# Where a kernel's tiles begin in SBUF: a constants tile wider by 32 bytes, and the t tiles in a pool of their own

## The chip, the cores and the metric

One core of one Trainium2 chip. The metric is the device time of one execution in microseconds (us). Three executions of the kernel before took 2665.67 to 2668.98 us, median 2666.57 us.

## What is computed

Two layers of one trunk. In each layer 256 latent rows and 256 context rows of 2048 channels are normalised and modulated, and one large projection feeds four mixers side by side. Cut to what matters:

```
for l in range(DEPTH):                                   # DEPTH = 2
    hx = modulate(rmsnorm(x, pre_g[l]), shift_x, scale_x)     # 256 x 2048
    hc = modulate(rmsnorm(ctx, pre_g[l]), shift_c, scale_c)   # 256 x 2048
    px = split_proj(hx @ w_in[l])                             # 2048 -> 14144 columns
    pc = split_proj(hc @ w_in[l])        # last layer: only the 320 columns of the keys
    ...                                  # latent attention, 2-D DFT, short convolution, gMLP
    br = jnp.einsum('bngw,gwd->bngd', ys, w_branch)           # 4 branches, 512 -> 2048
    merged = jnp.sum(sigmoid(gates) * br, axis=2)
    out = merged @ w_out                                      # 2048 -> 2048
    x = x + gate_x * rmsnorm(out, post_g[l])
```

Inputs and outputs are float32. The modulation vectors come from a further product of silu(c) and silu(c_ctx) with w_mod (2048 x 6144 per layer).

## The kernel before

Nearly all the time goes to matrix products with 128 x 512 tiles of weights. A weight is streamed from HBM in chunks of 256 rows by 512 columns (`raw`, 512 KB, issued on SP's queue, line 235). For each half of a chunk, ScalarE rounds the float32 numbers to float32r (`wh`, line 245) and VectorE subtracts to get the rest (`wl`, line 246). The inputs are kept split in the same way: `hh` and `hl` are 16 + 16 tiles of 128 x 512 that hold the modulated input, and `y` and `m` tiles hold the inputs of the smaller products. Each product is then the sum of three float32r matmuls: high by high, low by high, high by low. They are written in one place:

```
if mode == "f":
    c = slice(j * P, (j + 1) * P)
    mm(b, wh[kk][:, c], xh, start=first, stop=False)      # line 272
    mm(b, wh[kk][:, c], xl, start=False, stop=False)      # line 273
    mm(b, wl[kk][:, c], xh, start=False, stop=last)       # line 274
else:
    mm(b, xh, wh[kk], start=first, stop=False)            # line 276
    mm(b, xl, wh[kk], start=False, stop=False)            # line 277
    mm(b, xh, wl[kk], start=False, stop=last)             # line 278
```

The second argument of `mm` is the stationary operand, 128 columns of which are loaded into the array before the matmul (the weight loads, PEld). The third is the moving operand, whose 512 columns (256 or 320 in a few products) are streamed through it. So in mode "f" the input moves and the weights stand; in mode "t" the weights move and the input stands. Lines 502 to 504 are the same triple in mode "t" for cq and kv of layer 0, which are computed by quarters while the modulation is still being worked out. Layer 0 runs mostly in mode "f" (up to about 1700 us), layer 1 mostly in mode "t".

Float32 matmuls that aren't split (transposes against an identity, attention scores at lines 717 and 718, the modulation's own products at line 337) use operands of `cst`, `t`, `s`, `m` and `raw`.

The SBUF tiles are taken from pools, in this order:

```
pc, pv, pw, pb, ps = pool("pc"), pool("pv"), pool("pw"), pool("pb"), pool("ps", space=PSUM)
```

`pc` holds the constants, one tile `cst` of 1796 float32 columns (7184 bytes in each partition). `pv` holds small vectors. `pw` holds `raw` (5 buffers), `wh` (6) and `wl` (5). `pb` holds `s`, `g`, `m`, `t`, `y`, `hh`, `hl` and one accumulator `ma`, in this order. A tile lies at the same bytes of every partition, each buffer is rounded up to 32 bytes, and the next follows without a gap. So the size of everything ahead of a tile decides where it begins. One of the three `t` buffers must hold a tile with a border for the convolution, 4 x 2 x 258 columns, so each `t` buffer has 8256 bytes, 64 more than a multiple of 256.

Of the kernel before, what the change touches and what calls it, by code (L numbers as in the profile page):

```python
# [17 lines left out]
F32 = mybir.dt.float32  # L18
# [5 lines left out]
PSUM = bass.MemoryType.PSUM  # L24

P = 128
# [128 lines left out]
def backbone(ctx: ExitStack, tc: tile.TileContext, a, out):  # L155
    nc = tc.nc
    pool = lambda n, b=1, **k: ctx.enter_context(tc.tile_pool(name=n, bufs=b, **k))
    pc, pv, pw, pb, ps = pool("pc"), pool("pv"), pool("pw"), pool("pb"), pool("ps", space=PSUM)
    pd = pool("pd", space=bass.MemoryType.DRAM)

    mm = nc.tensor.matmul
# [3 lines left out]

    def big(tag, shape, dt=F32):
        n = {"m": 4, "y": 2, "t": 3}[tag]
        return pb.tile(shape, dt, tag=tag, name=tag, bufs=n)

    def small(shape, dt=F32):  # L170
        return pb.tile(shape, dt, tag="s", name="s", bufs=4)
# [144 lines left out]
    def mod_products(l, part, k0, nk):  # L316
# [4 lines left out]
        for s in range(KD // 4):  # L321
            off = moff[l][part * D + k0 * P] + s * 4 * P * n
            if n < W:
                raw = pw.tile([P, KC, W], F32, tag="raw", name="raw", bufs=NR).rearrange("p k n -> p (k n)")
            elif s % 2 == 0:
                raw = big("y", [P, 2048])
            else:
                raw = None
            if raw is not None:
                nc.sync.dma_start(raw.rearrange("p (c f) -> p c f", c=2),  # L330
                                  a[f"wm{l}"][off:off + 4 * P * n].rearrange("(c p f) -> p c f", c=2, p=P))
                rows = [raw[:, i * n:(i + 1) * n] for i in range(4)]
            else:
                two = [raw_chunk(a[f"wm{l}"], off + i * KC * P * n) for i in range(2)]
                rows = [two[i // KC][:, i % KC, :] for i in range(4)]
            for i in range(4):
                mm(b[i * 32:(i + 1) * 32, :], cvz[:, s * 4 + i, :], rows[i], start=s == 0, stop=s == KD // 4 - 1,  # L337
                   tile_position=(0, i * 32))
            yield
# [87 lines left out]

    nc.sync.dma_start(vecs[0], a["vec0"])
    ncst = sum(n for _, n in CONST.values())
    cst = pc.tile([P, ncst], F32, name="cst")  # L430
    nc.sync.dma_start(cst[:, :2 * P + 4], a["const"][:, :2 * P + 4])
    K = {n: cst[:, s:s + w] for n, (s, w) in CONST.items()}
    ident = K["ident"]
# [1 line left out]
    sinT = K["sinT"].rearrange("p (t n) -> p t n", t=2)  # L435

    xs = [big("m", [P, 4, 512]) for _ in range(4)]
    rows_of = {}
    for v, src in enumerate((a["x"], a["ctx"])):
        for i in range(2):  # L440
            rows_of[v, i] = x = big("y" if v + i == 2 else "t", [P, D])
            nc.sync.dma_start(x, src[i * P:(i + 1) * P, :])
# [104 lines left out]
        pending = to_modulate(k0, nk)  # L547
    for _ in pending:
        pass
    nc.sync.dma_start(cst[:, 2 * P + 4:], a["const"][:, 2 * P + 4:])  # L550
    nc.sync.dma_start(vecs[1], a["vec1"])
    for _ in products:
        pass
# [613 lines left out]
```

## Time and profile before

| | us |
|---|---|
| median of three executions | 2666.57 |
| the profiled execution | 2668.45 |
| its span, first to last instruction | 2666.6 |
| TensorE busy (PE) | 2613.7 |
| VectorE busy (DVE) | 1583.2 |
| ScalarE busy (ACT) | 1028.6 |

The profiled execution is 1.9 us above its span. A matmul's duration in the trace is its own latency, from its start to its modelled end; the next one starts before it ends. So durations of matmuls overlap, and the pace of TensorE is read from the starts of matmuls that follow each other, not from their durations. That distance from start to start is called the pitch below. At the full clock of 2.4 GHz, 512 columns take 213.3 ns.

### The profile page before, as it was taken

Reading aid. Unit: us, or ns where it says so; the run is one execution under the profiler, and the core shown is the slowest. Engines: PE = TensorE matmul, PEld = TensorE weight load, DVE = VectorE, ACT = ScalarE, POOL = GpSimd, SP = SyncE. Lnnn points to the kernel's source line nnn. Section 1 sums busy time; section 2 is a strip of 40 time slices with the busy share of each in tenths; the row PEclk is TensorE's granted clock in tenths of the full one; section 3 lists DMA queues with packets and bytes.
Section 4 is the critical chain, followed back from the end, with each engine's and each line's share of the span. In section 5 each row is a group of like instructions: output and inputs, shape, how many; then the busy total and the mean of one; then the engine's idle time right before and its main releaser. Section 6 shows DMA issues by size and latency. Waiting matters only on the chain.

```text
span 2666.6 us, 33124 instructions
## 1 busy us (share of the span) xinstructions
PE 2613.7 (98%) x11803; PEld 2103.3 (79%) x11803; DVE 1583.2 (59%) x3000; ACT 1028.6 (39%) x1881; POOL 11.7 (0%) x25
## 2 busy tenths in 40 slices
PE   6899999999999999999999999999999999999998
PEld 3578787888888888888888888789788888888886
DVE  4377555656666566754554336776555555656666
ACT  4234432222222222222222235565555444544554
POOL 0000000000000000000000000000000000000000
PEclk9999999999999999999999999999999999999999
DMA  8854234444444444444444226754445555566565
GB/s 304 324 184 142 80 111 142 153 148 150 149 147 148 141 150 150 146 155 158 150 163 145 93 92 210 247 172 137 140 150 174 189 192 194 184 207 199 185 218 205
DMA packets 127350, 448.62 MB, mean 168 GB/s; under 512 B 13920, under 2 KB 19216, under 8 KB 125264
## 3 DMA queue, kind: packets, MB, share of 16 engines
q1 hardware_dynamic: 124944, 433.11, 48.4%
q0 software_dynamic: 2240, 13.40, 1.4%
q8 instruction: 92, 1.51, 0.2%
q14 instruction: 74, 0.61, 0.1%
HBM read 442.23 MB, written 4.22 MB: 167 GB/s over the span
## 4 chain that ended last, share of the span: by engine, by line
PE 96%; DVE 2%; issue 1%; DMA 1%; ACT 0%; SPq 0%; DVEq 0%; ACTq 0%
PE acc L272 16%; PE acc L273 16%; PE acc L274 16%; PE acc L278 13%; PE acc L276 13%; PE acc L277 13%; PE acc L502 1%; PE acc L504 1%; PE acc L503 1%; PE acc L337 1%; PE mis L421 1%; PE mis L717 1%; PE mis L718 1%; DVE m L1075 0%; DMA raw<-in_wm 0%
## 5 line engine op out<-in xcount | busy, mean ns | idle before, releaser
L246 DVE TENSOR_TENSOR wl<-raw,wh 128x512 fp32r<-128x512 f32 (+1 forms) x1256 | 848.3, 682 | 764.8 <-PE acc L274 349.0
L245 ACT CAST wh<-raw 128x512 fp32r<-128x512 f32 (+1 forms) x1256 | 767.7, 615 | 1359.7 <-PE acc L273 818.0
L272 PE MATMUL acc<-hh,wh 128*128 128x512 f32 x1536 | 614.7, 400 | 0.6 <-DVE m L837 0.6
L273 PE MATMUL acc<-hl,wh 128*128 128x512 f32 x1536 | 607.4, 395 | 0.0
L274 PE MATMUL acc<-hh,wl 128*128 128x512 f32 x1536 | 607.2, 395 | 0.0
L276 PE MATMUL acc<-wh,hh 128*128 128x512 f32 (+1 forms) x1440 | 566.2, 393 | 0.0
L278 PE MATMUL acc<-wl,hh 128*128 128x512 f32 (+1 forms) x1440 | 559.6, 389 | 1.1 <-DVE wl L246 1.0
L277 PE MATMUL acc<-wh,hl 128*128 128x512 f32 (+1 forms) x1440 | 558.6, 388 | 0.0
L361 DVE SCALAR_TENSOR_TENSOR ma<-raw,cv,ma 128x512 f32<-128x512 f32 x420 | 298.2, 746 | 131.0 <-DMA raw<-in_wm 130.1
L272 PEld LDWEIGHTS acc<-hh,wh 128*128 128x128 f32 x1536 | 288.7, 188 | 72.1 <-issue 1.9
L273 PEld LDWEIGHTS acc<-hl,wh 128*128 128x128 f32 x1536 | 288.7, 188 | 70.1 <-issue 1.9
L274 PEld LDWEIGHTS acc<-hh,wl 128*128 128x128 f32 x1536 | 288.6, 188 | 69.6
L278 PEld LDWEIGHTS acc<-wl,hh 128*128 128x128 f32 x1440 | 270.5, 188 | 60.1 <-DVE wl L246 3.5
L277 PEld LDWEIGHTS acc<-wh,hl 128*128 128x128 f32 x1440 | 270.7, 188 | 56.8 <-issue 1.9
L276 PEld LDWEIGHTS acc<-wh,hh 128*128 128x128 f32 x1440 | 270.6, 188 | 56.0 <-issue 1.9
L272 PE MATMUL acc<-y,wh 128*128 128x512 f32 x256 | 101.7, 397 | 0.0
L273 PE MATMUL acc<-y,wh 128*128 128x512 f32 x256 | 101.2, 395 | 0.0
L274 PE MATMUL acc<-y,wl 128*128 128x512 f32 x256 | 101.2, 395 | 0.0
L502 PE MATMUL acc<-wh,hh 128*128 128x512 f32 (+1 forms) x128 | 48.4, 381 | 11.9 <-ACT wh L245 7.3
L274 PEld LDWEIGHTS acc<-y,wl 128*128 128x128 f32 x256 | 48.1, 188 | 11.6
L272 PEld LDWEIGHTS acc<-y,wh 128*128 128x128 f32 x256 | 48.1, 188 | 11.5
L273 PEld LDWEIGHTS acc<-y,wh 128*128 128x128 f32 x256 | 48.1, 188 | 11.5
(229 smaller groups left out, 1680.3 us busy)
## 6 DMA issues: line engine op xcount, KB each, us to landing
raw<-in_wi SPq DMA_DIRECT2D x432, 512.0 KB, 3.5
raw<-in_wm SPq DMA_DIRECT2D x168, 512.0 KB, 4.2
raw<-in_wo SPq DMA_DIRECT2D x104, 512.0 KB, 4.2
raw<-in_wb SPq DMA_DIRECT2D x64, 512.0 KB, 4.1
y<-in_wm SPq DMA_DIRECT2D x12, 1024.0 KB, 7.9
raw<-in_wi SPq DMA_DIRECT2D x16, 320.0 KB, 3.5
t<-row POOLq DMA_DIRECT2D x3, 1024.0 KB, 8.0
t<-in_x SPq DMA_DIRECT2D x2, 1024.0 KB, 6.4
```

The costliest lines, as they stand in the source:

```text
L245: nc.scalar.copy(h, raw[:, k, :])
L246: ve.tensor_tensor(l, raw[:, k, :], h.bitcast(F32), ALU.subtract)
L272: mm(b, wh[kk][:, c], xh, start=first, stop=False)
L273: mm(b, wh[kk][:, c], xl, start=False, stop=False)
L274: mm(b, wl[kk][:, c], xh, start=False, stop=last)
L276: mm(b, xh, wh[kk], start=first, stop=False)
L277: mm(b, xl, wh[kk], start=False, stop=False)
L278: mm(b, xh, wl[kk], start=False, stop=last)
L337: mm(b[i * 32:(i + 1) * 32, :], cvz[:, s * 4 + i, :], rows[i], start=s == 0, stop=s == KD // 4 - 1, tile_position=(0, i * 32))
L361: ve.scalar_tensor_tensor(s, raw[:, kk, :], cv[:, k, v:v + 1], s, ALU.mult, ALU.add)
L421: nc.tensor.transpose(dst[:, i * P:(i + 1) * P], x[:, k * P:(k + 1) * P], ident)
L502: mm(banks[i], ah(k, i), wh[kk], start=k == 4 * j, stop=False)
```

## The change

```
-    pc, pv, pw, pb, ps = pool("pc"), pool("pv"), pool("pw"), pool("pb"), pool("ps", space=PSUM)
+    pc, pv, pw, pb, pt, ps = pool("pc"), pool("pv"), pool("pw"), pool("pb"), pool("pt"), pool("ps", space=PSUM)
...
     def big(tag, shape, dt=F32):
         n = {"m": 4, "y": 2, "t": 3}[tag]
-        return pb.tile(shape, dt, tag=tag, name=tag, bufs=n)
+        return (pt if tag == "t" else pb).tile(shape, dt, tag=tag, name=tag, bufs=n)
...
-    cst = pc.tile([P, ncst], F32, name="cst")
+
+    cst = pc.tile([P, ncst + 8], F32, name="cst")
...
-    nc.sync.dma_start(cst[:, 2 * P + 4:], a["const"][:, 2 * P + 4:])
+    nc.sync.dma_start(cst[:, 2 * P + 4:ncst], a["const"][:, 2 * P + 4:])
```

The constants tile gets 8 more float32 columns that nothing reads, which moves all tiles behind it by 32 bytes. The `t` buffers move behind everything else, so that their odd size no longer moves `y`, `hh` and `hl`. No instruction is added, removed or moved: on every engine and queue the same instructions stand in the same order with the same waits. What differs is the byte at which tiles begin:

| tile | begins at, before | modulo 256 | begins at, after | modulo 256 |
|---|---|---|---|---|
| cst | 16512 | 128 | 16512 | 128 |
| raw | 26336 | 224 | 26368 | 0 |
| wh | 46816 | 224 | 46848 | 0 |
| wl | 59104 | 224 | 59136 | 0 |
| s, g | 69344, 77536 | 224 | 69376, 77568 | 0 |
| m | 85728 | 224 | 85760 | 0 |
| t | 118496 | 224, 32, 96 | 204544 | 0, 64, 128 |
| y | 143264 | 160 | 118528 | 0 |
| hh | 159648 | 160 | 134912 | 0 |
| hl | 192416 | 160 | 167680 | 0 |
| ma | 225184 | 160 | 200448 | 0 |

The buffers of `raw`, `wh`, `wl`, `s`, `g`, `m`, `y`, `hh` and `hl` are multiples of 256 bytes long, so all buffers of one name have the same remainder. The slices that matmuls read of them begin at multiples of 512 bytes within a tile.

## Rows read from the trace of the kernel before

**Rows 1.** The page: busy time by engine, and the chain that ended last.
```profile
PE 2613.7 (98%) x11803; PEld 2103.3 (79%) x11803; DVE 1583.2 (59%) x3000; ACT 1028.6 (39%) x1881; POOL 11.7 (0%) x25
...
PE 96%; DVE 2%; issue 1%; DMA 1%; ACT 0%; SPq 0%; DVEq 0%; ACTq 0%
```

**Rows 2.** Three stretches: busy us of each engine, granted clock, DMA share, GB/s.
```profile
0.00:160.00 160.00, 120.86 (x728) 76.68 (x729) 74.30 (x261) 57.24 (x132) 0.20 (x4) 0.95 0.80 297
160.00:1700.00 1540.00, 1539.40 (x6692) 1242.44 (x6691) 909.08 (x1629) 464.62 (x825) 5.69 (x10) 1.00 0.43 144
1700.00:2667.00 967.00, 953.44 (x4386) 784.19 (x4384) 599.85 (x1112) 506.74 (x925) 5.85 (x11) 0.99 0.57 186
```

**Rows 3.** Groups of matmuls by line and operands, with count, busy us, mean ns.
```profile
L272 PE MATMUL acc<-hh,wh 128*128 128x512 f32 x1536 | 614.7, 400 | 0.6 <-DVE m L837 0.6
L276 PE MATMUL acc<-wh,hh 128*128 128x512 f32 x1376 | 546.0, 397 | 0.0
L272 PE MATMUL acc<-y,wh 128*128 128x512 f32 x256 | 101.7, 397 | 0.0
L276 PE MATMUL acc<-wh,y 128*128 128x512 f32 x128 | 50.4, 394 | 0.0
L502 PE MATMUL acc<-wh,hh 128*128 128x512 f32 x64 | 26.9, 423 | 6.7 <-DVE hh L218 4.5 <-ACT wh L245 2.2
...
L502 PE MATMUL acc<-wh,hh 128*128 128x320 f32 x64 | 21.5, 338 | 5.2 <-ACT wh L245 5.2
...
L276 PE MATMUL acc<-wh,hh 128*128 128x320 f32 x64 | 20.2, 316 | 0.0
...
L272 PE MATMUL acc<-m,wh 128*128 128x512 f32 x40 | 16.3, 407 | 0.0
...
L272 PE MATMUL acc<-m,wh 128*128 128x256 f32 x24 | 6.9, 286 | 0.0
L276 PE MATMUL acc<-wh,m 128*128 128x512 f32 x16 | 6.2, 389 | 0.0
```

**Rows 4.** Timeline, hh and hl moving: first and last of 49 matmuls.
```profile
599.81 0.40 PE L273 MATMUL acc<-hl,wh 128*128 128x512 f32 x1
...
611.01 0.40 PE L273 MATMUL acc<-hl,wh 128*128 128x512 f32 x1
```

**Rows 5.** Timeline, hh and hl stationary: first and last of 49 matmuls.
```profile
1615.97 0.39 PE L276 MATMUL acc<-wh,hh 128*128 128x512 f32 x1
...
1626.95 0.39 PE L276 MATMUL acc<-wh,hh 128*128 128x512 f32 x1
```

**Rows 6.** Timeline, m stationary: first and last of 22 matmuls.
```profile
243.00 0.39 PE L276 MATMUL acc<-wh,m 128*128 128x512 f32 x1
...
247.76 0.39 PE L276 MATMUL acc<-wh,m 128*128 128x512 f32 x1
```

**Rows 7.** Timeline, narrow: 155 matmuls of 320 columns, then 47 of 256.
```profile
1841.12 0.31 PE L277 MATMUL acc<-wh,hl 128*128 128x320 f32 x1
...
1863.71 0.31 PE L278 MATMUL acc<-wl,hh 128*128 128x320 f32 x1
...
1864.29 0.28 PE L272 MATMUL acc<-m,wh 128*128 128x256 f32 x1
...
1869.81 0.28 PE L273 MATMUL acc<-m,wh 128*128 128x256 f32 x1
```

**Rows 8.** Timeline, unsplit float32: two matmuls of L717, then L718.
```profile
251.24 1.02 PE L717 MATMUL mis<-m,t 128*128 128x512 f32 x2
252.10 0.59 PE L718 MATMUL mis<-t 128*128 128x512 f32 x1
```

**Rows 9.** Groups on VectorE: count, busy us, mean ns, idle before.
```profile
L246 DVE TENSOR_TENSOR wl<-raw,wh 128x512 fp32r<-128x512 f32 x1216 | 830.3, 689 | 738.0 <-PE acc L274 344.7 <-PE acc L278 314.8 <-issue 53.2
...
L839 DVE TENSOR_TENSOR g<-g,acc 128x512 f32<-128x512 f32 x48 | 32.6, 682 | 3.0 <-PE acc L274 3.0
...
L219 DVE TENSOR_TENSOR y<-t,y 128x512 fp32r<-128x512 f32 x12 | 8.2, 681 | 0.0
```

## The prediction

> **What bounds the kernel now.** I read the page first. TensorE is busy for 2613.7 us of a span of 2666.6 us, and the chain that ended last lies on it for 96% [rows 1]. The reader is to see that nothing else comes near: VectorE has 1583.2 us, ScalarE 1028.6 us. Next the stretches [rows 2]. Only in the first 160 us does TensorE idle much (160.0 less 120.9, 39 us), while the DMA engines move 297 GB/s and the input is being normalised. From 160 to 1700 us it idles 0.6 us, from 1700 us to the end 13.6 us, most of that at the tail. Its granted clock is 1.00 there, which is 2.4 GHz. So after 160 us the time is the number of matmuls times the pitch at which they start, and a change of addresses matters if it changes the pitch.
>
> Then the timeline, for the pitch. A 512-column matmul can't take less than 213.3 ns at this clock. It takes more, and not always the same:
>
> - hh or hl moving, weights stationary: 611.01 less 599.81 is 11.20 us for 48 steps, 233.3 ns [rows 4].
> - weights moving, hh or hl stationary: 1626.95 less 1615.97 is 10.98 us for 48 steps, 228.8 ns [rows 5].
> - weights moving, m stationary: 247.76 less 243.00 is 4.76 us for 21 steps, 226.7 ns [rows 6].
>
> Rows 5 and rows 6 come from the same three source lines, with the same number of columns, at the same clock, and TensorE waits for nothing in either. Only the tile differs. Its remainder modulo 256 differs too: hh and hl begin at 160, m and the weights at 224. Moving at 160 costs 6.6 ns more than everything at 224; stationary at 160 costs 2.1 ns more. 6.6 ns is what 16 columns take at 2.4 GHz, 6.67 ns, and 16 float32 columns are 64 bytes, exactly the distance from 160 to 224. I take this as the sign that the pitch depends on where an operand begins.
>
> Two more pitches say what the surplus is like. With both at 224 and only 256 columns it is 5.52 us for 46 steps, 120.0 ns, and the columns need 106.7, so the surplus is 13.3 ns; with 320 columns it is 22.59 us for 154 steps, 146.7 ns against 133.3, again 13.3 [rows 7]. At 512 columns and 224 it is 226.7 less 213.3, the same 13.3. So it is paid once for each matmul, and it is two steps of 6.67 ns. The unsplit float32 matmuls don't pay it: from the first record of line 717 at 251.24 us to line 718 at 252.10 us are 0.86 us for two records, 430 ns each, which is two passes of 512 columns (426.7 ns) and 3 ns [rows 8]. So about 215 ns for a pass is possible, although those operands begin at 224 as well.
>
> **The change, part by part.** No instruction is added or moved, so there is nothing to cost but the addresses. First the counts [rows 3]. Each group of line 272, 276 or 502 stands for three lines. Moving hh, hl or y: 3 x (1536 + 256) = 5376. Stationary hh, hl or y, 512 columns: 3 x (1376 + 128 + 64) = 4704. Both at 224: 3 x (40 + 16) = 168. Narrow: 3 x (64 + 64 + 24) = 456. Together the 10,248 wide ones take 5376 x 233.3 + 4704 x 228.8 + 168 x 226.7 ns, that is 1254.2 + 1076.3 + 38.1 = 2368.6 us.
>
> What the pitch becomes with everything at 0 modulo 256 is shown by no row, since no split operand begins there. I bound it by the nearest rows. From above: 226.7 ns, if what counts is only that both operands share a remainder, which is then already the best case here. From below: 215 ns, the pass of the unsplit matmuls, if the whole surplus comes from odd starts. Between them lies a step. Both remainders of before, 160 and 224, are odd multiples of 32, so a moving row of 2048 bytes touches 33 pieces of 64 bytes where 32 would do. The surplus moves in steps of such a piece. An aligned start takes away that extra piece at least, which gives 226.7 less 6.7, that is 220.0 ns. For the stationary operand, 512 bytes in 9 pieces instead of 8, the second step may go as well, or not, since weight loads lie beside the running matmul. I take 220.0 ns.
>
> The sum at 220.0 ns: 10,248 x 0.2200 = 2254.6 us, which is 114.0 less. The 456 narrow ones give 6.67 ns each, 3.0 us. The 384 matmuls of lines 502 to 504 start while the first 160 us are still bound by other work; I count nothing for them: 192 x 8.8 ns and 192 x 6.7 ns, 3.0 us off. The profiled execution of 2668.5 us becomes 2668.5 - 114 = 2554.5 us, and since the median of before is 1.9 us under that execution, 2553 us.
>
> What the saving relies on is that the others keep up. From 160 to 1700 us VectorE is busy 909 of 1540 us and the DMA engines 0.43; after that 0.62, ScalarE 0.52 and the DMA engines 0.57 at 186 GB/s [rows 2]. With 5% less time these become at most 0.66 and 0.60, well below the 297 GB/s of the start. If this cover were gone, the time would stop falling where VectorE has no gap left, far below the range. VectorE itself doesn't care where its operands begin, as far as rows show: 689 ns with all at 224, 682 with one from PSUM, 681 with a t and a y tile at other remainders [rows 9]. So its cost, and ScalarE's, is counted unchanged. Transfers into raw also start elsewhere, but only the first 160 us wait for transfers, and I count nothing.
>
> The Trainium skill speaks against the change. Its page "TensorE: Matmul & The Clock Gate" (Part 2, the step on LDWEIGHTS) gives TensorE two independent SBUF read ports, so that loading the next weights takes nothing from the running matmul, and its section on the back-to-back issue gap makes the warm gap N/2.4 + 2.5 ns, an estimate of 216 ns at 512 columns, wherever operands lie. By that, addresses change nothing and the time stays at 2667 us. The trace disagrees: 233.3, 228.8 and 226.7 ns at one N [rows 4 to 6].
>
> **The rivals.**
>
> *Only the difference between the tiles goes* (226.7 ns). For it: rows 6 show this pitch where both operands share a remainder, and two streams that start in step may be all there is. Against it: nothing in the trace. 10,248 x 0.2267 = 2323.2 us, 45 less, 2621 us.
>
> *The whole surplus goes* (215 ns). For it: it is two pieces, and there are two operands with an odd start. Against it: the weights' piece may be hidden anyway. 10,248 x 0.215 = 2203.3, 165 less; the narrow ones add 5 and the early ones take 5 off. 2502 us.
>
> *Nothing changes.* hh, hl and y differ from m and the weights in one more way: they lie in the upper half of SBUF, from 143264 on, and hh and hl stay high (134912 on). If distance or half counts and not the remainder, 2665 us. Against it: the difference of exactly 64 bytes' worth of columns.
>
> *Slower.* The pitch fell by 6.6 ns when the start moved 64 bytes closer to the next multiple of 256. If it is the way to that multiple that costs, an operand at 0 has the longest way, 256 bytes against 32 at 224, and pays 3.5 such steps: 226.7 + 3.5 x 6.6 = 249.8 ns, and 10,248 x 0.2498 = 2560 us, 191 more, 2858 us. It decides from the point where the new pitch is over the present mean, 2368.6 us over 10,248, 231.1 ns. Against it: an aligned start that costs the most would be odd.
>
> **How the numbers follow.** 220 ns (217.5 to 223.5): 0.34. 226.7 ns: 0.28. 215 ns: 0.18. Nothing: 0.12. Slower: 0.08. A measurement of this kernel can tell about 0.2% from no change, since its executions lie within 0.12% of each other. The likeliest gives 2553 us; its own range is 2530 to 2590. The range that leaves out only the last two cases goes from 2490 (215 ns and a few us at the start) to 2640 (226.7 ns with some of it lost to waits). Faster 0.80, same 0.12, slower 0.08.
>
> **What would show it.** In the profile of the changed kernel, hh moving and hh stationary must have one pitch: 48 steps in 10.56 us where rows 4 have 11.20, and the same where rows 5 have 10.98. The 256-column triples must fall from 0.36 to 0.34 us. TensorE's busy time must fall by what the span falls, its idle time and the first 160 us stay as they are, and VectorE's 689 ns too. If the pitch falls and the span doesn't follow, waits at lines 272, 276 and 278 for ScalarE and VectorE must have grown. The prediction is wrong if hh and m still differ, if all stop at 226.7, or if the aligned pitch is above 231.1 ns.

## The result: 1.6% faster, and one pitch for all

The changed kernel took 2624.68 us (median of four executions, 2624.24 to 2627.07) against 2667.40 us for the kernel before, run beside it. The ratio is 0.9842, with a 95% interval from 0.9825 to 0.9859. That is 43 us, in the direction that was forecast but only 0.37 of the 114 us. It lies outside the range of the likeliest case (2530 to 2590 us), inside the wide one (2490 to 2640 us), and 4 us above the first rival (2621 us).

The page of the changed kernel, first its busy times, then the three stretches with busy us of each engine, granted clock, DMA share and GB/s:

```profile
PE 2572.2 (98%) x11803; PEld 2101.2 (80%) x11803; DVE 1578.1 (60%) x3000; ACT 1029.5 (39%) x1881; POOL 11.5 (0%) x25
```

```profile
0.00:160.00 160.00, 121.70 (x732) 77.42 (x733) 74.60 (x262) 57.66 (x132) 0.20 (x4) 0.94 0.81 299
160.00:1700.00 1540.00, 1537.78 (x6842) 1267.81 (x6841) 932.91 (x1691) 486.98 (x873) 7.56 (x14) 1.00 0.46 150
1700.00:2667.00 967.00, 912.77 (x4233) 755.93 (x4231) 570.58 (x1049) 484.87 (x877) 3.74 (x7) 0.99 0.55 175
```

TensorE's busy time fell by 41.5 us from [rows 1], and the span by 41.3, from 2666.6 to 2625.3. The first 160 us are as they were [rows 2]. From 160 to 1700 us the window holds 6842 matmuls where it held 6692. The last window reaches 42 us past the end of the changed kernel, so its shares are low; TensorE idles 12.5 us of the 925.3 us that are left there. So the whole gain lies in the pace of TensorE.

The timeline of the changed kernel: hh and hl moving, hh and hl stationary (first and last of 49 matmuls each), then m (first and last of 22):

```profile
599.85 0.39 PE L274 MATMUL acc<-hh,wl 128*128 128x512 f32 x1
...
610.73 0.40 PE L274 MATMUL acc<-hh,wl 128*128 128x512 f32 x1
...
1599.96 0.39 PE L277 MATMUL acc<-wh,hl 128*128 128x512 f32 x1
...
1610.84 0.39 PE L277 MATMUL acc<-wh,hl 128*128 128x512 f32 x1
```

```profile
241.69 0.39 PE L274 MATMUL acc<-m,wl 128*128 128x512 f32 x1
...
246.45 0.39 PE L278 MATMUL acc<-wl,m 128*128 128x512 f32 x1
```

Both long stretches take 10.88 us for 48 steps, 226.7 ns, where [rows 4] had 233.3 and [rows 5] 228.8. The m tiles take 4.76 us for 21 steps, 226.7 ns, exactly what they had [rows 6], although they too moved, from 224 to 0. All three now have the pitch of the one that was best before, and none has less. The narrow matmuls (256 and 320 columns) did not change: 120.0 ns with 256 columns (47 steps from 1828.70 to 1834.34 us) and 146.6 ns with 320 (175 steps from 1802.89 to 1828.55 us), where [rows 7] have 120.0 and 146.7.

### The profile page after: what moved, and what is told of

Same layout as the page of the kernel before. It is cut to its first block, busy times and chain, and to the rows that moved or that the text cites. A ratio compares the mean times of both kernels' runs of the same rounds, so it can differ in the third digit from the quotient of the medians.

```text
span 2625.3 us, 33124 instructions
## 1 busy us (share of the span) xinstructions
PE 2572.2 (98%) x11803; PEld 2101.2 (80%) x11803; DVE 1578.1 (60%) x3000; ACT 1029.5 (39%) x1881; POOL 11.5 (0%) x25
## 5 line engine op out<-in xcount | busy, mean ns | idle before, releaser
L272 PE MATMUL acc<-hh,wh 128*128 128x512 f32 x1536 | 605.9, 394 | 1.2 <-DVE m L838 0.6
L274 PE MATMUL acc<-hh,wl 128*128 128x512 f32 x1536 | 598.0, 389 | 0.0
L273 PE MATMUL acc<-hl,wh 128*128 128x512 f32 x1536 | 597.9, 389 | 0.0
```

## Experiments

Two theories stood after the result. **S:** what counts is the distance modulo 256 between a matmul's moving and its stationary operand, and distance 0 is best. **M:** each operand's own start counts, and a multiple of 256, or of 64, is best.

### The t tiles last, without the 8 columns

```
-    cst = pc.tile([P, ncst + 8], F32, name="cst")
+    cst = pc.tile([P, ncst], F32, name="cst")
```

> One half of the change alone: the t tiles go to the last pool, the constants tile keeps its 1796 columns. All operands of split matmuls then begin at 224 modulo 256, none at a multiple of 64. Theory S (what counts is the distance modulo 256 between the moving and the stationary operand, and equal remainders give 226.7 ns): one pitch of 226.7 ns, the time of the changed kernel, 2625 us within 4. Theory M (a start at a multiple of 256, or of 64, is what helps): the pitch stays where it was for some pairs, and the time lies between 2640 and 2667 us.

Measured: 2626.27 us, ratio to the kernel before 0.9842 (0.9825 to 0.9858). Its timeline, hh and hl moving, then stationary, first and last of 49 each:

```profile
620.00 0.39 PE L274 MATMUL acc<-hh,wl 128*128 128x512 f32 x1
...
630.88 0.39 PE L274 MATMUL acc<-hh,wl 128*128 128x512 f32 x1
...
1599.90 0.39 PE L277 MATMUL acc<-wh,hl 128*128 128x512 f32 x1
...
1610.78 0.39 PE L277 MATMUL acc<-wh,hl 128*128 128x512 f32 x1
```

10.88 us for 48 steps both times, 226.7 ns, with every operand at 224. This half has the whole gain. No operand of a split matmul begins at a multiple of 256, or even of 64.

### The 8 columns, with the t tiles where they were

```
-        return (pt if tag == "t" else pb).tile(shape, dt, tag=tag, name=tag, bufs=n)
+        return pb.tile(shape, dt, tag=tag, name=tag, bufs=n)
```

> The other half alone: 8 more columns in the constants tile, the t tiles stay where they were. Weights and m then begin at 0 modulo 256, y, hh and hl at 192, so all are multiples of 64, and the distance from the weights to hh is the same as before, 192. Theory S: the pitches of before, 233 ns with hh moving and 229 ns with hh stationary, and the time of before, 2667 us within 4. Theory M with multiples of 64: 226.7 ns or less everywhere and 2625 us or less; with multiples of 256: only the operand at 0 is cured, between 2625 and 2667 us.

Measured: 2666.74 us, ratio 1.0000 (0.9991 to 1.0009). Its timeline, hh moving (48 matmuls), then stationary (49):

```profile
599.93 0.39 PE L272 MATMUL acc<-hh,wh 128*128 128x512 f32 x1
...
610.90 0.40 PE L274 MATMUL acc<-hh,wl 128*128 128x512 f32 x1
...
1631.85 0.39 PE L276 MATMUL acc<-wh,hh 128*128 128x512 f32 x1
...
1642.84 0.39 PE L276 MATMUL acc<-wh,hh 128*128 128x512 f32 x1
```

10.97 us for 47 steps is 233.4 ns, 10.99 for 48 is 229.0: the pitches of before, with the weights at 0 and hh at 192. All operands of split matmuls begin at multiples of 64 here, and the weights at multiples of 256, but neither pitch changed. So M falls, for 64 and for 256.

### Inputs at multiples of 256, weights 32 bytes off

To the first experiment's kernel a gap is added between the pool of the weights and that of the inputs:

```
-    pc, pv, pw, pb, pt, ps = pool("pc"), pool("pv"), pool("pw"), pool("pb"), pool("pt"), pool("ps", space=PSUM)
+    pc, pv, pw, pg, pb, pt, ps = pool("pc"), pool("pv"), pool("pw"), pool("pg"), pool("pb"), pool("pt"), pool("ps", space=PSUM)
+    nc.vector.memset(pg.tile([P, 8], F32, name="gap"), 0.0)
```

> The t tiles last and the constants tile as before, and a gap of 32 bytes behind the weights' pool. y, hh, hl and m then begin where they do in the changed kernel, at multiples of 256, but raw, wh and wl begin at 224 again, so that each pair is 32 or 224 bytes apart modulo 256. One small memset is added. Theory S with the map's pitches (233.4 ns at distance 32, 233.2 at 224): all 10,248 wide matmuls at 233.3 ns, 2391 us where the kernel before has 2369, so 22 us slower than before, 2689 us within 5. Theory M (the input's start at a multiple of 256 is what helped): mode f at 227 to 230 ns and a time below 2660 us.

Measured: 2686.32 us, ratio 1.0075 (1.0058 to 1.0092), 0.75% slower than before. Its timeline, hh moving, then stationary, 48 matmuls each (lines are one higher here):

```profile
601.82 0.39 PE L273 MATMUL acc<-hh,wh 128*128 128x512 f32 x1
...
612.79 0.40 PE L275 MATMUL acc<-hh,wl 128*128 128x512 f32 x1
...
1639.86 0.40 PE L279 MATMUL acc<-wl,hh 128*128 128x512 f32 x1
...
1650.83 0.40 PE L278 MATMUL acc<-wh,hl 128*128 128x512 f32 x1
```

10.97 us for 47 steps, 233.4 ns, in both modes, as S forecast. hh, hl, y and m lie at the same addresses as in the changed kernel; 32 bytes between them and the weights cost 62 us against it.

Narrow matmuls don't follow S. First and last of 48 with 256 columns, m moving at distance 32:

```profile
1868.68 0.28 PE L273 MATMUL acc<-m,wh 128*128 128x256 f32 x1
...
1874.17 0.28 PE L275 MATMUL acc<-m,wl 128*128 128x256 f32 x1
```

5.49 us for 47 steps is 116.8 ns, less than the 120.0 ns at distance 0 in the changed kernel and in [rows 7]. With 320 columns the pitch is 146.7 ns here, at distance 224, as it is at 64 [rows 7], and 146.6 ns at 0 in the changed kernel.

### A map of starts

A small kernel times each pair of starts by itself:

```
for c in LET:                      # moving at 0, 32, ... 224: mvA ... mvH
    for d in LET:                  # stationary at 0, 32, ... 224: stA, suA ... stH, suH
        run(f"p{c}{d}", mv[c], (st[d], su[d]))     # 48 matmuls, the two stationary tiles in turn
```

> A kernel of matmuls alone, nothing of the model is computed and the output is zeros and one product: float32r, 512 columns, 48 in a row for each of 64 pairs of a moving operand that begins at 0, 32, ... 224 modulo 256 and two stationary ones that begin at 0, 32, ... 224 and take turns. Then, with all at 0: stationary operands of 64 and of 32 columns, moving ones of 256 and 384, one stationary operand used again and again, bfloat16, and unsplit float32. Theory S: the pitch depends on moving less stationary modulo 256 alone, 226.7 ns at distance 0, 233.3 at 192 and 228.8 at 64. Theory M: it depends on each start by itself, with steps at multiples of 64. If the weight load beside the running matmul makes the 13.3 ns that are left, they shrink with 64 and 32 stationary columns and in bfloat16; if it is a fixed cost of a float32r matmul they stay.

Its timeline: the first matmul of each segment with moving C (64 bytes), and of what follows segment HH. Each segment has 48 matmuls, so the pitch is the distance to the next row divided by 48.

```profile
210.59 0.39 PE L54 MATMUL pCA<-mvC,stA 128*128 128x512 f32 x1
...
221.58 0.40 PE L54 MATMUL pCB<-mvC,stB 128*128 128x512 f32 x1
...
232.78 0.39 PE L54 MATMUL pCC<-mvC,stC 128*128 128x512 f32 x1
...
243.66 0.39 PE L54 MATMUL pCD<-mvC,stD 128*128 128x512 f32 x1
...
254.85 0.40 PE L54 MATMUL pCE<-mvC,stE 128*128 128x512 f32 x1
...
266.06 0.39 PE L54 MATMUL pCF<-mvC,stF 128*128 128x512 f32 x1
...
277.29 0.39 PE L54 MATMUL pCG<-mvC,stG 128*128 128x512 f32 x1
...
288.45 0.40 PE L54 MATMUL pCH<-mvC,stH 128*128 128x512 f32 x1
...
299.65 0.40 PE L54 MATMUL pDA<-mvD,stA 128*128 128x512 f32 x1
...
734.10 0.39 PE L54 MATMUL pHH<-mvH,stH 128*128 128x512 f32 x1
...
744.98 0.40 PE L54 MATMUL colh<-mvA,stA 128*64 128x512 f32 x1
...
756.02 0.40 PE L54 MATMUL colq<-mvA,stA 128*32 128x512 f32 x1
...
767.14 0.28 PE L54 MATMUL nhalf<-mvA,stA 128*128 128x256 f32 x1
```

With moving less stationary modulo 256 as the distance, the eight segments give:

| distance | 0 | 32 | 64 | 96 | 128 | 160 | 192 | 224 |
|---|---|---|---|---|---|---|---|---|
| segment | CC | CB | CA | CH | CG | CF | CE | CD |
| us for 48 | 10.88 | 11.20 | 10.99 | 11.20 | 11.16 | 11.23 | 11.21 | 11.19 |
| ns | 226.7 | 233.3 | 229.0 | 233.3 | 232.5 | 234.0 | 233.5 | 233.1 |

The kernel before had distance 192 in mode f and 64 in mode t: 233.3 and 228.8 there [rows 4, 5], 233.5 and 229.0 here, with no other engine at work. HH, with both at 224, takes 10.88 us like CC, so the start itself doesn't count. All 64 segments agree: the eight pairs of one distance lie within 1 ns of each other. S holds as it was stated, for 512 columns. At distance 0 what is left over 213.3 ns doesn't shrink with smaller weight loads: with 64 stationary columns the pitch is 11.04 / 48, 230.0 ns, and with 32 it is 11.12 / 48, 231.7 ns. It neither shrinks nor stays, which neither case of the expectation had.

### Finer distances, and bfloat16

> A kernel of matmuls alone, nothing of the model is computed. The moving operand begins at 0, 4, 8, ... 252 bytes modulo 256, the two stationary ones at 0: 64 distances, float32r, 512 columns, 48 in a row each. Then stationary operands of 64 and of 32 columns, and bfloat16, each at distances 0, 32, ... 224. If streaming and weight load collide by their phase, the pitch has one narrow best distance, and it may lie off 0, with less than 226.7 ns and down to 216 ns; a version with that distance would beat the changed kernel. If multiples of 32 are the grain, it is flat in steps of 32 and 226.7 ns is the least. In bfloat16 the pitch stays at 216 ns at every distance if half the bytes leave room for the load, and varies if the collision is one of places.

The moving operand is a slice of one tile, shifted by 4 bytes from segment to segment (`mz[:, i:i + W]`), the stationary ones begin at 0. First matmuls of segments, each with the first of the segment behind it, 48 matmuls later; FA, halfF and quarF have the distance 160 with 128, 64 and 32 stationary columns:

```profile
86.60 0.40 PE L44 MATMUL qAF<-mz,sta 128*128 128x512 f32 x1
...
98.11 0.40 PE L44 MATMUL qAG<-mz,sta 128*128 128x512 f32 x1
...
477.62 0.40 PE L44 MATMUL qFA<-mz,sta 128*128 128x512 f32 x1
...
488.87 0.39 PE L44 MATMUL qFB<-mz,sta 128*128 128x512 f32 x1
...
702.00 0.39 PE L44 MATMUL qHE<-mz,sta 128*128 128x512 f32 x1
...
712.88 0.40 PE L44 MATMUL qHF<-mz,sta 128*128 128x512 f32 x1
...
801.63 0.39 PE L44 MATMUL halfF<-mz,sta 128*64 128x512 f32 x1
...
812.74 0.40 PE L44 MATMUL halfG<-mz,sta 128*64 128x512 f32 x1
...
890.73 0.39 PE L44 MATMUL quarF<-mz,sta 128*32 128x512 f32 x1
...
901.80 0.40 PE L44 MATMUL quarG<-mz,sta 128*32 128x512 f32 x1
...
955.02 0.38 PE L44 MATMUL bfD<-mb,sba 128*128 128x512 bf16 x1
...
965.38 0.38 PE L44 MATMUL bfE<-mb,sba 128*128 128x512 bf16 x1
```

At 20 bytes (AF) it is 11.51 us, 239.8 ns, and 132, 196 and 244 bytes are as slow, up to 239.9. At 240 bytes (HE) it is 10.88 us, 226.7 ns, no better than 0, and 28, 60, 156, 236 and 252 bytes are within 0.3 ns of that. No distance is below 226.7 ns, so none of the 64 promises wide matmuls faster than the changed kernel's.

With fewer stationary columns the distance matters less. At the eight distances 0, 32, ... 224 the pitch goes from 226.7 to 234.4 ns with 128 columns, from 228.4 to 232.6 with 64 and from 230.1 to 233.3 with 32. At distance 0 fewer columns are slower, but at 160 they are faster: 11.25 us for 128 (234.4 ns), 11.11 for 64 (231.5) and 11.07 for 32 (230.6).

In bfloat16 (bf segments, here at 96 bytes) 48 steps take 10.36 us, 215.8 ns, and all eight distances tried, in steps of 32 bytes, lie within 0.3 ns of that.

### Which load is in the way

> A kernel of matmuls alone, nothing of the model is computed. Two moving operands (at 0 and at 32, 64, ... 224 modulo 256) and two stationary ones with the same starts take turns. In the segments named own each matmul has a moving and a stationary operand with the same start, and the weight load beside it, which is the next matmul's, has the other start. In those named next it is the other way round. If the moving stream collides with the load of the next matmul's weights, which runs beside it in the trace, own has the slow pitches (229 to 234 ns) and next has 226.7. If it is a matmul's own two operands that count, it is the reverse. Then stationary operands that are 256, 512, ... 65536 bytes further on than the moving one's remainder: 226.7 ns in all if 256 is the whole period.

First matmuls of segments, 48 apart; from farB to end there are 8 segments:

```profile
43.22 0.39 PE L45 MATMUL nextB<-mvA,stB 128*128 128x512 f32 x1
...
54.26 0.39 PE L45 MATMUL ownC<-mvA,stA 128*128 128x512 f32 x1
...
198.52 0.39 PE L45 MATMUL farB<-mvA,far 128*128 128x512 f32 x1
...
285.56 0.39 PE L45 MATMUL end<-mvA,stA 128*128 128x512 f32 x1
```

nextB has 11.04 us, 230.0 ns. No segment of either kind came down to 226.7, so neither theory of this run holds alone. The far segments are clear: 87.04 us for 384 steps, 226.7 ns, with one of the two stationary operands 512, 1024, ... 65536 bytes further on. So these multiples of 256 change nothing.

> A kernel of matmuls alone, nothing of the model is computed. The run before it had no segment at 226.7 ns, so neither a matmul's own stationary operand alone nor the next one's alone explained it. Here one operand in eight is out of step and all others begin at 0: in the segments named stat it is a stationary operand, in those named move a moving one, at 32, 64, ... 224. The pitch is read by place in the group of eight. If a stream collides with the load of the next weights, a stationary operand out of step lengthens the matmul ahead of its own (place 7 of 8) and one out of step in moving lengthens its own (place 8). If a matmul's own two operands collide, both lengthen place 8. If the surplus is shared among neighbours, several places are over 226.7 ns.

First and last of the 96 matmuls of three segments: one stationary operand in eight off by 128 bytes, one moving operand in eight off by 64, one moving off by 128:

```profile
98.38 0.40 PE L40 MATMUL statE<-mvA,stA 128*128 128x512 f32 x1
...
120.08 0.40 PE L40 MATMUL statE<-mvA,stE 128*128 128x512 f32 x1
...
208.34 0.39 PE L40 MATMUL moveC<-mvA,stA 128*128 128x512 f32 x1
...
230.40 0.40 PE L40 MATMUL moveC<-mvC,suA 128*128 128x512 f32 x1
...
252.81 0.39 PE L40 MATMUL moveE<-mvA,stA 128*128 128x512 f32 x1
...
274.44 0.40 PE L40 MATMUL moveE<-mvE,suA 128*128 128x512 f32 x1
```

Over 95 steps the pitches are 228.4, 232.2 and 227.7 ns. One operand out of step in eight therefore costs between 8 and 44 ns for the eight (8 x 1.0 and 8 x 5.5 ns over 226.7). The 44 ns of moveC are far more than one matmul at the slowest pitch could add, 13 ns, so its neighbours are slowed too.

By place, as the expectation asked, in means of the last eleven groups: the matmul out of step itself (place 8) is longer than 226.7 ns in all 14 segments, 228.4 to 237.0 ns. The one ahead of it (place 7) is longer in some stat segments (statF 236.6) and not in others (statC 226.0, statG 225.6), and in moveC others of the eight reach 241.0. So neither of the first two cases holds as it was written: the one would lengthen place 7 in every stat segment, the other place 8 alone. The third case, a surplus shared among neighbours, fits. Which of the loads is in the way was not settled.

## Why the prediction was off in size

**The bound, the counts and the cover were right.** The gain is TensorE's pitch, only there, and VectorE, ScalarE and the DMA engines kept up: DMA share from 0.43 to 0.46 in the long stretch, VectorE from 909 to 933 us of 1540, TensorE's idle time from 0.6 to 2.2 us [rows 2].

**The term that was mis-sized is the pitch of 220.0 ns; it is 226.7.** The step was the count of 64-byte pieces: an operand that begins at an odd multiple of 32 touches one more, and an aligned start was to save that one "at least". It saves nothing; "all stop at 226.7" was one of the prediction's own signs of being wrong. With both operands at 224 the pitch is the same as with both at 64 or at 0 (map, e1). 10,248 wide matmuls with 6.7 ns each are 68.7 us, which is the error of 72 us but for 3 us. The 3.0 us of the narrow matmuls, sized by the same step, came out as nothing.

**The reading behind it failed too.** From [rows 4 to 6] I took that a start at 160 costs more than one at 224, as a property of each operand, because 6.6 ns matched the 64 bytes between them. The same rows fit the distance between the two operands: 192, 64 and 0. Two numbers in the rows spoke against the reading. The 2.1 ns of a stationary operand at 160 are no step of 6.67 ns. And the 320-column matmuls of [rows 7] have hh or hl standing at 160, not both operands at 224, yet their surplus is the same 13.3 ns. That both operands share a remainder was written down as the first rival (2621 us, 0.28), with nothing against it. It came out within 4 us.

**The other cases.** "Nothing" rested on the half of SBUF that hh and hl lie in; they stayed there, and their pitch fell. "Slower" rested on the way to the next multiple of 256; the changed kernel, with all at 0, and e1, with all at 224, have one pitch, so this way doesn't count. A slower side does exist, by distance, and e3 is on it. "The whole surplus" would have needed less than 226.7 ns at 512 columns somewhere, and none of 64 distances has it.

**The page.** The Trainium skill ("TensorE: Matmul & The Clock Gate", Part 2, the step on LDWEIGHTS) says that loading the next tile's weights doesn't steal SBUF read bandwidth from the running matmul. The bfloat16 segments show nothing against it, 215.8 ns at all eight distances. The float32r ones speak against it, 226.7 to 234.4 ns at the same eight distances and less spread with fewer weight columns, but no run shows that reads of SBUF are what is shared.

**What stays open.** That weight load and moving stream collide is argued from the dependence on their distance, from its smaller size with fewer weight columns and from bfloat16's lack of it; no run shows the collision itself, and the last two runs show that neighbours are slowed as well. Why 256 columns are faster at distance 32 than at 0, and why 320 columns have one pitch at 0, 64 and 224, is open; no run maps their distances. What makes the 13.3 ns that are left at the best distance is not known. Of the 45 us that 226.7 ns for all would give, the span shows 41.3. Most of the missing 4 us stands in the trace of the changed kernel: from 160 us on, the mean pitch of the 512-column matmuls, taken where the next one starts within 260 ns, is 226.9 ns with hh, hl or y moving (5319 steps) and 227.2 with them standing (4460 steps), over 3 us more than 226.7 for all. Why it is above 226.7 is not known.

## What to carry to other kernels

Where a stream of float32r matmuls of 512 columns sets the time, read its pitch from the starts in the timeline for each pair of tiles, and compare pairs by the distance of their starts modulo 256, not by each start. Give the tiles that are moved and the tiles that stand the same remainder; which one makes no difference, and one tile of an odd size between them is enough to lose it. For other widths measure first: with 256 columns distance 32 beat distance 0, 116.8 against 120.0 ns. Before a size is taken from a row, ask which other quantity changes in the same row: here one more column in a small table, the difference, would have shown that a second reading fits as well.

## What the runs showed of the hardware that was not expected

In a stream of like matmuls, a float32r matmul of 512 columns and 128 stationary ones takes 226.7 to 239.9 ns at full clock, by the distance between its two operands modulo 256 bytes. Steps of 4 bytes matter: 226.7 ns at 0 and 240 bytes, 239.8 at 20. Fewer stationary columns make it slower at distance 0 (226.7 ns with 128, 230.0 with 64, 231.7 with 32) and faster at 160 (234.4, 231.5, 230.6). Narrow ones differ: 120.0 ns at distance 0 and 116.8 at 32 with 256 columns, 146.6 to 146.7 at three distances with 320. bfloat16 keeps 215.8 ns at the eight distances tried.
